# One reciprocal per attention head, head sums of squares on either engine, and weight halves split as separate chains, in a two-layer hybrid trunk

## The chip, the core and the metric

The kernel runs on one core of one Trainium2 chip. A core has five engines, each with its own instruction queue: TensorE (PE, matrix products, the weight load shown as PEld), VectorE (DVE), ScalarE (ACT), GpSimd (POOL) and SyncE (SP, which here only starts transfers). The metric is the device time of one execution in microseconds (us), lower being better.

## The reference

The program is a decoder trunk of two layers on one sequence of 512 tokens with 1024 features, all in fp32. Each layer does the following.

```python
h = rmsnorm(x, norm_g)
p = h @ w_in                                   # 1024 -> 3488 columns, split into 15 parts
q = rope(rmsnorm(rmsnorm(cq) @ w_uq))          # A: latent attention, 4 heads, causal
k, v_a from rmsnorm(ckv) @ w_ukv and kr
o_b = c_b * short_conv(c_c * c_h)              # B: gated width-3 convolution
o_c = sg_u * (tril(sg_w) @ layernorm(sg_v) + sg_b)   # C: chunked spatial gate
qd, kd = rope(rmsnorm(mq)), rope(rmsnorm(mk))  # D: block-sparse attention, 4 heads
o_d = moba(qd, kd, mv)
y = concat(o_a * silu(g_a), o_b * silu(g_b), o_c * silu(g_c), o_d * silu(g_d))
x = x + y @ w_out
```

With 512 tokens and blocks of 256, the block choice of group D selects every earlier block, so it is causal attention too. The per-head norms of q, k, mq and mk need a sum of squares over 64 or 96 values for each token and head. The softmax of each head needs one row sum for each token, and its reciprocal.

## The kernel before, in words

**Precision.** TensorE multiplies in fp32r, a shortened form. Each fp32 operand is split into a high half (the value cast to fp32r) and a low half (value minus high half), and each product is three matmuls: high by high, high by low, low by high (`mm3`, L277). In the names, `whi_` and `wlo_` are the halves of a weight block, `hTh`/`hTl` those of the transposed normalised input, `yTh`/`yTl` those of the gated outputs.

**A planner writes the order.** The Python code runs once, when the program is built, and decides in which order each engine gets its instructions. Class `Order` (L70) has a clock for TensorE (`now`) and one for each of ScalarE (`A`), VectorE (`V`), GpSimd (`G`) and the transfers (`D`). Work is written as generators, "chains" (L162), held in a heap with a due time and a priority (lower goes first). A chain emits an instruction when its inputs are at most 300 ns ahead of `now` (L144, L169), advances the engine's clock by a cost formula (L176 to L194), and goes on. A "lazy" chain also holds back while the engine's own clock is ahead. On the chip, each engine then works strictly through its list, and semaphores hold it where an input is late. Every VectorE, ScalarE and GpSimd instruction is issued in `_emit`, so the profile names line 174 for all of them, and 204 for all matmuls. One reads by tile names.

**TensorE's order of the stages.** In a layer, `main` (L1574) goes through `SEQ` (L364): the low-rank columns (`cq` tiles, weights `c0` to `c3`), `sq`, `ga`, `kv`, then the feature blocks `su`, `gc`, `ch`, `cc`, `gd`, `cb`, `gb`, with the heads' score and value matmuls set between them, and last the output projection. The latter is done in seven block products with sums of weight blocks (`ZPROD`, L46: b11, t3, b21, t4, t2, t1, b22), each of 24 matmuls for an output tile (`prod` and `left` in `main`; results leave through `z_out`, L1544, which adds them to the residual tiles `xr`). The product t1 goes into the bank in which t2's result stood (`oy`), so it starts only when VectorE has added that to `xr`. The left operands of these products are sums of outputs, too, made by VectorE (`ys`, `suml`, `u`).

**Weight blocks ("units").** Each weight block is 128 x 1024 values. `load_units` (L386) loads it on SyncE's queue into a raw tile. There are two such slots (`NRAW`), and the second of each pair of output blocks uses the slots of the rotary scratch. SyncE works in order, so a load that waits for a free slot holds back the loads and copies after it. `split_units` (L417) casts each half of the columns to `whi_` on ScalarE or VectorE, by the planner's clocks, and subtracts on VectorE to get `wlo_`:

```python
yield from c2.act(A.activation, hi, raw, AF.Copy)
...
yield from c2.dve(V.tensor_tensor, lo, raw, hi.bitcast(F32), op=ALU.subtract)
```

For all units but the first four, high and low are made one after the other, first half then second half, and the raw slot is given back (`u.raw_slots.put`) and the unit declared ready at the end. `uq` and `ukv` also carry a gain per row (`split_scaled`, L268). The first four units have the low halves as chains of their own (`low_half`, L456). A product asks for a unit with `unit` (L464), waits for the whole of it, and marks the next `AHEAD` = 4 units as wanted, which lifts the hold on their splits. The sums of weight blocks for t1 to t4 are built in DRAM (`t_sums`, L344): SyncE copies one block, GpSimd's queue adds the other with an accumulating transfer.

**Per-head norms.** `head_means` (L829) squares a whole 128-token tile of q, k, mq or mk on ScalarE into a scratch tile and reduces it to four numbers on VectorE (tiles `squares...` and `rs_...`). When the fourth token tile is done (`L.todo`), GpSimd makes the reciprocal roots.

**Softmax.** For each head and each of its four query tiles, `soft_chain` (L1272) does, on VectorE, the scaled and masked scores and their row minimum, on ScalarE the exponential with the row sum as accumulator, on VectorE the reciprocal of one column, and on ScalarE or VectorE the normalisation. `pt_block` (L1296) then transposes the normalised rows on TensorE, and the halves are split (`pha`, `pla`, `phd`, `pld`).

Of the kernel before, what the change touches and what calls it, by code (L numbers as in the profile page):

```python
# [33 lines left out]
AHEAD = 4  # L34
NWARM, FILL, FILLEND = 6, 0.9, 15000.0
MIXT, MIXLAG, ROWT, COLT = 42000.0, 2000.0, 36000.0, 17500.0
KSPLIT = 6
# [179 lines left out]
def hybrid_trunk(ctx: ExitStack, tc: tile.TileContext, x, positions, norm_g, w_c, w_f, w_t, w_o, mla_q_norm_g,  # L217
# [199 lines left out]
    def split_units(i0, i1):  # L417
        for u in order[i0:i1]:
            ch = Chain(o)
            if u.name != "c0_0":  # L420
                yield from ch.wait(u.loaded)
            u.hi, u.lo = yield from u.slots.get(ch, u.name)
            n = u.a * u.b
            gain = {"uq": 2 * int(u.name[-1]), "ukv": 4 + int(u.name[-1])}.get(u.name[:-2])
            if gain is not None:
                yield from ch.wait(pc_ev)
            for i in range(2):
                if u.name == "c0_0":
# [7 lines left out]
                hi, lo, raw = u.hi[:, sl], u.lo[:, sl], u.raw[:, sl]  # L436
                if gain is not None:
# [33 lines left out]
    LOAD_HOOKS = {}  # L471

# [136 lines left out]
    class Layer:  # L609
        pass  # L610
# [31 lines left out]
    for l in range(DEPTH):  # L642
# [8 lines left out]
        L.todo = {n: NT for n in ("q", "k", "mq", "mk")}  # L651
# [177 lines left out]
    def head_means(ch, L, n, t, z):  # L829

        w = z.shape[2]
        sq = (yield from t2S.get(ch, f"squares{n}{t}"))[:, :4 * w].rearrange("p (h d) -> p h d", h=4)
# [3 lines left out]
        L.todo[n] -= 1  # L836
# [51 lines left out]
    def low_chain(L, t, a, t0, slots):  # L888
# [36 lines left out]
    def q_chain(L, t, q_ps, t0):  # L925
# [13 lines left out]
        if L.todo["q"]:  # L939
            return  # L940
# [11 lines left out]
    def kv_chain(L, t, kv_ps, t0):  # L952
# [23 lines left out]
        if L.todo["k"]:  # L976
# [242 lines left out]
    def mqk_chain(nm):  # L1219
        def f(L, t, a, t0, put):  # L1220
# [11 lines left out]
            if L.todo[nm]:  # L1232
# [39 lines left out]
    def soft_chain(H, qt, s, t0):  # L1272
# [3 lines left out]
        mn = sm.tile([P, 4], F32, tag="mn", name=f"mn{H.name}{qt}")  # L1276
# [3 lines left out]
                          scalar=BIG, op0=ALU.add, op1=ALU.min, accum_out=mn[:, 0:1])  # L1280
# [79 lines left out]
    def heads(L, grp, Vt, prep, qk):  # L1360
        prev = None
        ya_box, ya_left, ya_ev = None, None, None
        for h in range(4):
# [3 lines left out]
            H.rs, H.rs_ev = L.rs[rn], L.rs_ev[rn]  # L1367
            H.soft = [Event() for _ in range(NT)]
# [205 lines left out]
    def main():  # L1574
        m = Chain(o)

        def tok(L, n, width, t, dst, us, k0=0, k1=KT):

            for k in range(k0, k1):
# [61 lines left out]
        def seven(L):  # L1641
# [72 lines left out]
        for L in layers:  # L1714
# [10 lines left out]
            for t in L.torder if l else ():  # L1725
                a = yield from accS.get(m, f"cq{t}_{l}")
                yield from tok(L, "c", 416, t, a[:, 0:416], us)
# [8 lines left out]
            for n in SEQ:  # L1736
                if n in TOKS:
                    us = []
                    for ts in PAIRS.get((n, l), range(NT)):
# [4 lines left out]
                        for k in range(KT):  # L1744
                            for t in ts:
                                yield from tok(L, n, 512, t, a[t], us, k, k + 1)
# [166 lines left out]
```

## Time and profile before

| what | value |
|---|---|
| time, median of 3 runs | 494.73 us (493.85 to 496.37) |
| the profiled execution's own time | 494.88 us |
| its span in the profile | 493.2 us |
| TensorE busy | 486.3 us, 99% |
| VectorE busy | 389.6 us, 79% |
| ScalarE busy | 296.6 us, 60% |
| GpSimd busy | 93.9 us, 19% |
| granted TensorE clock | 1.00 |
| instructions | 7371 |

Span is the time from the first to the last instruction in the profile; the execution's own time is 1.7 us longer. A row of the timeline gives start and duration in us, engine, line, operation, the tile written and the tiles read, the shape, the number of instructions that stand together in the row, and in brackets the idle time of the engine just before it with what ended it. A row of the groups gives the total, and the mean in ns of one instruction. Durations of matmuls overlap, so their pace is read from the starts.

### The profile page before, as it was taken

The page shows a single profiled execution, that of the slowest core. Times are in us where ns is not written, and L with a number is a line of the kernel's source. Part 1 is how long each engine was busy: PE and PEld are TensorE (multiplying, and loading weights), DVE is VectorE, ACT ScalarE, POOL GpSimd, SP SyncE. Part 2 cuts the span into 40 slices and gives each one's busy share as a digit, 9 for nine tenths or more (in the row PEclk, how much of TensorE's full clock was granted, in tenths as well). Part 3 has the DMA queues.
Part 4 walks back from the last instruction along what each step waited for, and adds up shares of the span by engine and source line. Part 5 has one row for each costly group of instructions (what it writes and reads, how often), then busy time and mean ns, then how long its engine had stood idle before and what let it go on. Part 6 is the DMA issues. An engine that isn't in the chain of part 4 may idle for free.

```text
span 493.2 us, 7371 instructions
## 1 busy us (share of the span) xinstructions
PE 486.3 (99%) x2456; PEld 412.8 (84%) x2456; DVE 389.6 (79%) x922; ACT 296.6 (60%) x729; POOL 93.9 (19%) x164
## 2 busy tenths in 40 slices
PE   8999999999999999999999999999999999999997
PEld 7988888888888888888789988888888888888886
DVE  3588788679899888889896777787988878665982
ACT  6788437566557666457476753576746777534730
POOL 7835422100131000000131127040004010000000
PEclk9999999999999999999999999999999999999999
DMA  8525322536493829995564352639149275574562
GB/s 261 192 70 153 121 86 86 128 120 158 152 231 120 182 65 298 238 396 201 181 205 130 90 201 63 202 91 166 64 179 246 88 207 114 182 260 171 204 207 86
DMA packets 36557, 81.33 MB, mean 165 GB/s; under 512 B 6806, under 2 KB 18600, under 8 KB 36264
## 3 DMA queue, kind: packets, MB, share of 16 engines
q1 hardware_dynamic: 28048, 72.48, 43.2%
q0 software_dynamic: 8448, 8.39, 11.3%
q8 instruction: 19, 0.31, 0.3%
q14 instruction: 18, 0.15, 0.1%
q10 hardware_dynamic: 24, 0.01, 0.0%
HBM read 73.00 MB, written 24.64 MB: 198 GB/s over the span
## 4 chain that ended last, share of the span: by engine, by line
PE 86%; DVE 4%; DMA 4%; ACT 2%; issue 1%; SPq 1%; POOL 0%; ACTq 0%; DVEq 0%; POOLq 0%
PE kv L204 10%; PE sq L204 9%; PE cq L204 5%; PE oy L204 5%; PE ch L204 5%; PE cb L204 5%; PE gd L204 4%; PE gb L204 4%; PE cc L204 4%; PE ga L204 4%; PE su L204 4%; PE gc L204 3%; PE sa L204 3%; PE ox L204 2%; PE oz L204 2%; PE sd L204 2%
## 5 line engine op out<-in xcount | busy, mean ns | idle before, releaser
L356 POOL DMA_DIRECT2D t<-in_w_o_dram x16 | 17.2, 1146 | 72.4 <-DMA t<-t 46.5
L174 ACT ACTIVATE pa<-pa,mna 128x256 f32<-128x256 f32 (+3 forms) x48 | 25.8, 549 | 8.2 <-DVE mna L174 8.0
L174 ACT ACTIVATE pd<-pd,mnd 128x256 f32<-128x256 f32 (+3 forms) x50 | 26.7, 549 | 3.5 <-DVE mnd L174 3.5
L204 PE MATMUL kv<-whi_kv,hTh 128*128 128x512 f32 x64 | 27.0, 421 | 0.0
L174 ACT ACTIVATE pha<-pTa 128x512 fp32r<-128x512 f32 (+3 forms) x32 | 14.0, 438 | 21.0 <-PE pTa L204 20.8
L174 ACT ACTIVATE phd<-pTd 128x512 fp32r<-128x512 f32 (+3 forms) x32 | 13.7, 435 | 19.6 <-PE pTd L204 19.5
L204 PE MATMUL kv<-whi_kv,hTl 128*128 128x512 f32 x64 | 25.2, 393 | 0.0
L204 PE MATMUL kv<-wlo_kv,hTh 128*128 128x512 f32 x64 | 25.0, 391 | 0.0
L204 PE MATMUL cq<-whi_c,hTh 128*128 128x416 f32 x64 | 20.9, 371 | 0.8 <-ACT hTh L174 0.8
L174 DVE TENSOR_TENSOR pla<-pTa,pha 128x512 fp32r<-128x512 f32 (+3 forms) x32 | 15.4, 485 | 7.5 <-ACT pha L174 7.5
L174 DVE TENSOR_TENSOR wlo_t<-raw_t,whi_t 128x512 fp32r<-128x512 f32 x32 | 21.0, 685 | 0.0
L174 DVE TENSOR_TENSOR pld<-pTd,phd 128x512 fp32r<-128x512 f32 (+3 forms) x32 | 15.3, 486 | 7.2 <-ACT phd L174 7.1
L204 PE MATMUL cq<-wlo_c,hTh 128*128 128x416 f32 x64 | 20.0, 359 | 0.0
L204 PE MATMUL cq<-whi_c,hTl 128*128 128x416 f32 x64 | 19.8, 355 | 0.0
L174 DVE CUSTOM_DVE_ANT_0 pa<-sa,maskb,rs_q 128x512 f32<-128x512 f32 (+3 forms) x32 | 17.0, 545 | 3.3 <-PE pTa L204 2.1
L174 DVE CUSTOM_DVE_ANT_0 pd<-sd,maskb,rs_mq 128x512 f32<-128x512 f32 (+3 forms) x32 | 16.8, 544 | 2.7 <-PE pTd L204 2.5
L204 PE MATMUL sq<-yTh,hTh 128*128 128x512 f32 x48 | 18.9, 394 | 0.0
L204 PE MATMUL sq<-yTl,hTh 128*128 128x512 f32 x48 | 18.7, 390 | 0.0
L204 PE MATMUL sq<-yTh,hTl 128*128 128x512 f32 x48 | 18.7, 389 | 0.0
L174 ACT ACTIVATE whi_t<-raw_t 128x512 fp32r<-128x512 f32 x32 | 18.2, 618 | 0.6 <-DMA raw_t<-t 0.6
L174 DVE TENSOR_TENSOR wlo_b<-raw_b,whi_b 128x512 fp32r<-128x512 f32 x24 | 15.9, 686 | 1.7 <-ACT whi_b L174 1.7
L174 POOL TENSOR_TENSOR rs_mk<-rs_mk,nhalf 128x16 f32<-128x16 f32 x2 | 6.2, 3112 | 56.3 <-DVE rs_mk L174 56.3
(415 smaller groups left out, 1739.6 us busy)
## 6 DMA issues: line engine op xcount, KB each, us to landing
t<-in_w_o_dram POOLq DMA_DIRECT2D x16, 512.0 KB, 8.5
raw_t<-t SPq DMA_DIRECT2D x16, 512.0 KB, 5.0
raw_b<-in_w_o_dram SPq DMA_DIRECT2D x12, 512.0 KB, 4.7
raw_sq<-in_w_t_dram SPq DMA_DIRECT2D x8, 512.0 KB, 4.0
raw_kv<-in_w_t_dram SPq DMA_DIRECT2D x8, 512.0 KB, 3.6
t<-in_w_o_dram SPq DMA_DIRECT2D x8, 512.0 KB, 5.8
t<-t SPq DMA_DIRECT2D x8, 512.0 KB, 5.2
ys<-ysc SPq DMA_DIRECT2D x14, 256.0 KB, 5.5
```

The lines of the kernel that those rows point to most:

```text
L174: f(*a, **k)
L204: f(*a, **k)
L356: nc.gpsimd.dma_start(z_src(l, n, j), quad(l, b, j), accum_op=ALU.add, max_dma_last_dim=1024)
```

## The change

There are three parts.

1. In `soft_chain`, the row sums of a head's four query tiles lie side by side in one tile (`H.mn`). The query tile whose exponential is the last issues one reciprocal of 128 x 4, and all four normalisations wait for it (`H.rc_ev`).
2. `head_means` waits in the planner until its instructions are nearly due, and then chooses by the planner's clocks: if ScalarE's clock is behind VectorE's (`HMEAN` = 0), four squares with accumulator on ScalarE, one for each head, and no reduce; otherwise the old pair. `L.last` counts the tiles in place of `L.todo`.
3. In `split_units`, every unit's low halves are chains of their own, with priority 5 (the first four units keep -5). While the planner's VectorE clock is more than `VSLACK` = 300 ns ahead of `now` and the unit is more than `URGENT` = 2 units behind the one that TensorE is at, the subtraction is put off. Consumers wait for the half that they use, and the raw slot is given back when both halves are done. `split_scaled` is no longer used there: the gain goes through the same code.

```diff
-AHEAD = 4
+AHEAD, URGENT, VSLACK = 4, 2, 300.0
-KSPLIT = 6
+KSPLIT, HMEAN = 6, 0.0
...
                 if gain is not None:
                     c = gain + (i if u.a == 2 else 0)
-                    yield from split_scaled(c2, hi, lo, raw, pcol[:, c:c + 1])
-                    continue
+                    g = pcol[:, c:c + 1]
                 if o.clk["V"] + 600.0 < o.clk["A"] and u.idx > 3 or u.idx == 0 and i == 0:
-                    yield from c2.dve_fast(V.tensor_copy, hi, raw)
+                    if g is None:
+                        yield from c2.dve_fast(V.tensor_copy, hi, raw)
+                    else:
+                        yield from c2.dve(V.tensor_scalar, hi, raw, g, None, op0=ALU.mult)
                 else:
-                    yield from c2.act(A.activation, hi, raw, AF.Copy)
-                if u.idx < 4:
-                    o.set(u.high[i], c2.t)
-                    o.spawn(low_half(u, i, c2, lo, raw, hi), None, LOPRIO)
-                    continue
-                yield from c2.dve(V.tensor_tensor, lo, raw, hi.bitcast(F32), op=ALU.subtract)
-            if u.idx < 4:
-                continue
-            ch.t = c2.t
-            u.raw_slots.put(ch)
-            o.set(u.ready, ch.t)
-
-    def low_half(u, i, ch, lo, raw, hi):
-        yield from ch.dve(V.tensor_tensor, lo, raw, hi.bitcast(F32), op=ALU.subtract)
+                    yield from c2.act(A.activation, hi, raw, AF.Copy, scale=1.0 if g is None else g)
+                o.set(u.high[i], c2.t)
+                o.spawn(low_half(u, i, c2, lo, raw, hi, g), None, LOPRIO if u.idx < 4 else 5)
+                ch.t = max(ch.t, c2.t - LAT)
+
+    def low_half(u, i, ch, lo, raw, hi, g):
+        while o.clk["V"] > o.now + VSLACK and u.idx > at[0] + URGENT:
+            yield o.now + 100.0
+        ch.t = max(ch.t, o.now)
+        if g is None:
+            yield from ch.dve(V.tensor_tensor, lo, raw, hi.bitcast(F32), op=ALU.subtract)
+        else:
+            yield from ch.dve(V.scalar_tensor_tensor, lo, in0=raw, scalar=g, in1=hi.bitcast(F32),
+                              op0=ALU.mult, op1=ALU.subtract)
         o.set(u.half[i], ch.t)
...
     def unit(ch, name, half=None):
         u = units[name]
+        at[0] = max(at[0], u.idx)
...
     class Layer:
-        pass
+        def last(self, n, ch):
+
+            self.got[n].append(ch.t)
+            ch.t = max(self.got[n])
+            return len(self.got[n]) < NT
...
     def head_means(ch, L, n, t, z):
 
         w = z.shape[2]
+        while max(ch.t, o.clk["A"]) > o.now + SLACK:
+            yield max(ch.t, o.clk["A"]) - SLACK
+        if o.clk["A"] + HMEAN < o.clk["V"]:
+            for h in range(4):
+                yield from ch.act(A.activation, junk[:, :w], z[:, h, :], AF.Square, scale=w ** -0.5,
+                                  accum_out=L.rs[n][:, t, h:h + 1])
+            return
...
-        L.todo[n] -= 1
...
-        uq_h, uq_l = yield from unit(ch, f"uq_{l}")
         for k in range(2):
+            uq_h, uq_l = yield from unit(ch, f"uq_{l}", k)
...
-        yield from ch.act(A.activation, pr, pr, AF.Exp, scale=-1.0, bias=mn[:, 0:1], accum_out=mn[:, 1:2])
-        yield from ch.dve(V.reciprocal, mn[:, 2:3], mn[:, 1:2])
+        yield from ch.act(A.activation, pr, pr, AF.Exp, scale=-1.0, bias=mn[0], accum_out=mn[1])
+        H.exps.append(ch.t)
+        if len(H.exps) == NT:
+            ch.t = max(H.exps)
+            yield from ch.dve(V.reciprocal, H.mn[:, 2, :], H.mn[:, 1, :])
+            o.set(H.rc_ev, ch.t)
+        yield from ch.wait(H.rc_ev)
         if o.clk["A"] + 0.4 * n < o.clk["V"]:
-            yield from ch.act(A.activation, pr, pr, AF.Copy, scale=mn[:, 2:3])
+            yield from ch.act(A.activation, pr, pr, AF.Copy, scale=mn[2])
         else:
-            yield from ch.dve_fast(V.tensor_scalar, pr, pr, mn[:, 2:3], None, op0=ALU.mult)
+            yield from ch.dve_fast(V.tensor_scalar, pr, pr, mn[2], None, op0=ALU.mult)
...
-                if len(us) == k // 2:
-                    us.append((yield from unit(m, f"{n}{k // 2}_{L.l}")))
-                wh, wlo = us[k // 2]
+                wh, wlo = yield from unit(m, f"{n}{k // 2}_{L.l}", k % 2)
...
-                    if (n, kk // 2) not in us:
-                        us[n, kk // 2] = yield from unit(m, f"{n}{kk // 2}_{l}")
-                    wh, wlo = us[n, kk // 2]
+                    wh, wlo = yield from unit(m, f"{n}{kk // 2}_{l}", kk % 2)
...
-                    wh, wlo = yield from unit(m, f"{n}_{l}")
                     for k in range(KT):
+                        wh, wlo = yield from unit(m, f"{n}_{l}", k // 4)
```

More of the change, by code (lines that the diff above doesn't have):

```diff
@@ L471, in hybrid_trunk @@
     LOAD_HOOKS = {}
+    at = [0]
     def shared(slots, n):
@@ L650, in hybrid_trunk @@
         L.qd, L.kd, L.vd = Event(), Event(), [Event() for _ in range(NT)]
-        L.todo = {n: NT for n in ("q", "k", "mq", "mk")}
+        L.got = {n: [] for n in ("q", "k", "mq", "mk")}
         L.stat = [Event() for _ in range(NT)]
@@ L938, in q_chain @@
         yield from head_means(ch, L, "q", t, Q[:, t])
-        if L.todo["q"]:
+        if L.last("q", ch):
             return
@@ L975, in kv_chain @@
         yield from head_means(ch, L, "k", t, K[:, t, :, 0:64])
-        if L.todo["k"]:
+        if L.last("k", ch):
             return
@@ L1231, in f @@
             yield from head_means(ch, L, nm, t, dst[:, t])
-            if L.todo[nm]:
+            if L.last(nm, ch):
                 return
@@ L1275, in soft_chain @@
         pr = yield from pS[qt].get(ch, f"p{H.name}{qt}")
-        mn = sm.tile([P, 4], F32, tag="mn", name=f"mn{H.name}{qt}")
+        if H.mn is None:
+            H.mn = sm.tile([P, 3, NT], F32, tag="mn", name=f"mn{H.name}")
+        mn = [H.mn[:, i, qt:qt + 1] for i in range(3)]
         yield from ch.wait(H.rs_ev)
@@ L1279, in soft_chain @@
                           scale=H.rs[:, qt, H.h:H.h + 1],
-                          scalar=BIG, op0=ALU.add, op1=ALU.min, accum_out=mn[:, 0:1])
+                          scalar=BIG, op0=ALU.add, op1=ALU.min, accum_out=mn[0])
         sS.put(ch)
-        yield from ch.act(A.activation, pr, pr, AF.Exp, scale=-1.0, bias=mn[:, 0:1], accum_out=mn[:, 1:2])
-        yield from ch.dve(V.reciprocal, mn[:, 2:3], mn[:, 1:2])
+        yield from ch.act(A.activation, pr, pr, AF.Exp, scale=-1.0, bias=mn[0], accum_out=mn[1])
[5 more added lines that the diff above has]
+        yield from ch.wait(H.rc_ev)
         if o.clk["A"] + 0.4 * n < o.clk["V"]:
-            yield from ch.act(A.activation, pr, pr, AF.Copy, scale=mn[:, 2:3])
+            yield from ch.act(A.activation, pr, pr, AF.Copy, scale=mn[2])
         else:
-            yield from ch.dve_fast(V.tensor_scalar, pr, pr, mn[:, 2:3], None, op0=ALU.mult)
+            yield from ch.dve_fast(V.tensor_scalar, pr, pr, mn[2], None, op0=ALU.mult)
         H.pr[qt] = pr
@@ L1367, in heads @@
             H.rs, H.rs_ev = L.rs[rn], L.rs_ev[rn]
+            H.mn, H.exps, H.rc_ev = None, [], Event()
             H.soft = [Event() for _ in range(NT)]
@@ L1575, in main, with tok @@
         m = Chain(o)
-        def tok(L, n, width, t, dst, us, k0=0, k1=KT):
+        def tok(L, n, width, t, dst, k0=0, k1=KT):
             for k in range(k0, k1):
@@ L1726, in main @@
                 a = yield from accS.get(m, f"cq{t}_{l}")
-                yield from tok(L, "c", 416, t, a[:, 0:416], us)
+                yield from tok(L, "c", 416, t, a[:, 0:416])
                 o.spawn(low_chain(L, t, a, o.now + PELAT, accS))
@@ L1745, in main @@
                             for t in ts:
-                                yield from tok(L, n, 512, t, a[t], us, k, k + 1)
+                                yield from tok(L, n, 512, t, a[t], k, k + 1)
                         for t in ts:
```

1 line of the change is left out of this document (added).

## The prediction

> **What bounds the kernel now.** I read the busy line of the page first, then its waits of TensorE, then the windows, then the timeline wherever TensorE's cadence breaks.
>
> ```profile
> span 493.2 us, 7371 instructions
> PE 486.3 (99%) x2456; PEld 412.8 (84%) x2456; DVE 389.6 (79%) x922; ACT 296.6 (60%) x729; POOL 93.9 (19%) x164
> ...
> PE 86%; DVE 4%; DMA 4%; ACT 2%; issue 1%; SPq 1%; POOL 0%; ACTq 0%; DVEq 0%; POOLq 0%
> ```
>
> TensorE is busy for 99% of the span, and the chain that ended last is 86% TensorE. A matmul's own duration overlaps its neighbours, so the useful number is the distance from start to start. These two rows of TensorE's timeline stand next to each other in the output stage:
>
> ```profile
> 215.65 0.39 PE L204 MATMUL oz<-whi_b,yTl 128*128 128x512 f32 x1
> 215.88 0.39 PE L204 MATMUL ox<-whi_t,yTh 128*128 128x512 f32 x1
> ```
>
> A 512-column matmul starts 0.23 us after the one before it, and this cadence holds nearly everywhere. The change keeps the set of TensorE instructions, so only starts later than the cadence can be won back. The waits of TensorE by releaser are all there is beside small re-fills:
>
> ```profile
> PE warm L1827 <- DVE ones L1825: 1.1, 1, 1.1
> PE cq L204 <- ACT hTh L174: 0.8, 3, 0.3
> PE hT L204 <- DVE hTl L174: 0.7, 1, 0.7
> PE kv L204 <- ACT Q L174: 0.4, 1, 0.4
> ```
>
> They come to 3.0 us (columns: total, times, longest). What is left to win is small; what can be lost has no such bound. The windows (20 us each: width, then busy time of PE, PEld, DVE, ACT, POOL, then clock, DMA share, GB/s) tell where a second engine is full:
>
> ```profile
> 20.00:40.00 20.00, 19.57 (x106) 17.42 (x106) 15.68 (x43) 16.92 (x63) 11.75 (x25) 1.00 0.29 88
> 200.00:220.00 20.00, 20.00 (x92) 16.52 (x91) 17.03 (x29) 10.44 (x19) 0.00 (x0) 1.00 1.01 332
> 220.00:240.00 20.00, 19.91 (x87) 15.95 (x86) 19.37 (x39) 12.79 (x29) 0.00 (x0) 1.00 0.59 200
> ```
>
> VectorE is full (19.37 of 20) in layer 0's output stage, ScalarE is nearly so at 20 to 40 us, and the DMA engines are full at 200 to 220 us. There the order of instructions decides. Elsewhere both have room.
>
> **The change part by part.** I compared the instruction order of both kernels on each engine. TensorE, GpSimd and SyncE hold the same instructions; VectorE has 58 fewer (924 to 866) and ScalarE 54 more (621 to 675).
>
> *Reciprocals.* 64 of one column become 16 of four columns.
>
> ```profile
> L174 DVE RECIPROCAL mnd<-mnd 128x1 f32<-128x1 f32 x32 | 4.6, 154 | 0.6 <-ACT pd L174 0.6
> ```
>
> That takes 48 x 0.154 = 7.4 us off VectorE at most. It adds a wait: the normalisation of every query tile now waits for the last of the head's four exponentials. Behind it stand the normalised rows that TensorE transposes. In both orders TensorE has other matmuls between a head's last score and its first transpose: summed at the cadence, 4.4 us at least before, 5.1 at least after. The chain that must fit in is row minimum, exponential, reciprocal, normalisation; no wait on `pa` or `pd` stands among TensorE's waits. From the rows of those forms (VectorE's `pa<-sa,maskb,rs_q` 0.55 on average, normalisation on ScalarE 0.72, an exponential taken as long as that at 0.72, reciprocal 0.15) it is 2.1 us, with the accumulator read of the rows below 2.4. Cost nothing; if the cover went, it would cost what exceeds 5.1.
>
> ```profile
> L174 ACT ACTIVATE pa<-pa,mna 128x512 f32<-128x512 f32 x11 | 7.9, 719 | 5.3 <-DVE mna L174 5.3
> L174 DVE CUSTOM_DVE_ANT_0 pa<-sa,maskb,rs_q 128x512 f32<-128x512 f32 (+3 forms) x32 | 17.0, 545 | 3.3 <-PE pTa L204 2.1
> ```
>
> *Sums of squares.* 22 of the 32 square-and-reduce pairs become four small squares with accumulator on ScalarE. The reduce leaves VectorE, the large square leaves ScalarE, and 88 small ones of 64 or 96 columns come. The nearest rows:
>
> ```profile
> L174 DVE TENSOR_REDUCE rs_q<-squaresq 128x4 f32<-128x384 f32 x8 | 4.3, 543 | 0.1
> L174 ACT ACTIVATE squaresq<-Q 128x384 f32<-128x384 f32 x8 | 4.1, 520 | 0.0
> L174 ACT ACTIVATION_READ_ACCUMULATOR junk<-cq 128x1 f32 x24 | 5.1, 210 | 0.0
> L174 ACT ACTIVATE junk<-cq 128x128 f32<-128x128 f32 x8 | 2.2, 278 | 0.1
> L174 ACT ACTIVATE junk<-cq 128x32 f32<-128x32 f32 x8 | 1.6, 199 | 0.1
> ```
>
> Up to 22 x 0.54 = 12 us leave VectorE. A small square costs between 0.199 and 0.278, with its read (0.210) some 0.45 us. So at most 88 x 0.45 - 22 x 0.52 = 28 us more go to ScalarE, which then stands near 325 of 493 us. [...] For the end I take nothing, because ScalarE idles 40% of the span; ScalarE falling behind is a rival below.
>
> *Low halves and their order.* The split of a weight block into high and low halves is now four chains; consumers wait per half. The amount of work is equal; what moves is when. Four places answer.
>
> (a) First stage, ScalarE's timeline and then TensorE's:
>
> ```profile
> 13.21 0.99 ACT L174 ACTIVATE whi_c<-raw_c 128x416 fp32r<-128x416 f32 x2 [0.85 <-DMA raw_c<-in_w_c_dram]
> ...
> 14.51 0.67 ACT L174 ACTIVATE hTh<-xT,pg 128x512 fp32r<-128x512 f32 x1
> 15.23 1.03 PE L204 MATMUL cq<-whi_c,hTh 128*128 128x416 f32 x4 [0.25 <-ACT hTh L174]
> ```
>
> Two `whi_c` halves stand ahead of the `hTh` that TensorE waits for. In the new order only one does. That would put `hTh` half of 0.99 - 0.10 earlier (0.45), but the one before it is anchored to the landing of raw_c at 13.2, and another small square stays. I take -0.35, between 0 and -0.8 (the whole waiting time on `hTh`).
>
> (b) The first key/value product waits for ScalarE's copy of q:
>
> ```profile
> 33.87 0.51 ACT L174 ACTIVATE Q<-q 128x384 f32<-128x384 f32 x1
> 33.62 0.39 PE L204 MATMUL sq<-yTh,hTl 128*128 128x512 f32 x1
> 34.43 0.50 PE L204 MATMUL kv<-whi_ukv,cTh 128*128 128x512 f32 x1 [0.42 <-ACT Q L174]
> ```
>
> 34.43 - 33.62 - 0.23 = 0.58 us lost. In the new order that copy stands ahead of several squares and casts, and adding ScalarE's rows up to it puts it near 32, before TensorE wants its bank. I take -0.58; ends -0.58 and +1.0 (should four small squares, 4 x 0.45 less 0.8 of shadow, get ahead of it).
>
> (c) The first low half of the late `sq` weight block:
>
> ```profile
> 42.84 0.69 DVE L174 TENSOR_TENSOR wlo_sq<-raw_sq,whi_sq 128x512 fp32r<-128x512 f32 x1
> 42.77 0.80 PE L204 MATMUL sq<-whi_sq,hTh 128*128 128x512 f32 x1
> 43.41 0.40 PE L204 MATMUL sq<-wlo_sq,hTh 128*128 128x512 f32 x1
> ```
>
> 43.41 - 42.77 - 0.23 = 0.41 lost. Afterwards its raw slot is freed some 2 us earlier, so both halves are done by 41.8 by the sum of VectorE's rows. I take -0.41; ends -0.41 and 0.
>
> (d) Output stage of layer 0. TensorE's product t1 adds into a bank that VectorE must read first (`xr<-xr,oy`). VectorE has no gap between these two:
>
> ```profile
> 221.62 0.68 DVE L174 TENSOR_TENSOR xr<-xr,ox 128x512 f32<-128x512 f32 x1
> 222.21 0.42 DVE L174 TENSOR_TENSOR ys<-ys 128x256 f32<-128x256 f32 x1
> ...
> 237.33 1.38 DVE L174 TENSOR_TENSOR xr<-xr,oy 128x512 f32<-128x512 f32 x2
> 237.59 0.39 PE L204 MATMUL oy<-whi_t,suml 128*128 128x512 f32 x1
> 238.07 0.50 PE L204 MATMUL oy<-whi_t,sumh 128*128 128x512 f32 x1
> ```
>
> The next instruction starts 0.59 us after one of 512 columns; the one of 256 takes 0.335 in a row. Before, 31 instructions stand from the first `xr` (included) to the second, 15.7 us by these distances, as measured (237.33 - 221.62 = 15.71). After, 33 stand there: two `wlo_t` and one `suml` of 512 and one `ys` of 256 come in, two `wlo_b` of 512 go behind: +0.60 + 0.335 = +0.94. TensorE already waits here (238.07 - 237.59 - 0.23 = 0.25), so all of it shows: +0.94. The ends are 0 (if VectorE had slack, or enters this stretch earlier) and +1.9 (if the last `suml`, also later, adds its own stall).
>
> (e) Elsewhere low halves are made nearer to their use. Matmul time between the last result VectorE needs and the first use falls from about 20 us to 13 to 17 in the feature products, and for the third `kv` block of layer 0 from 10.7 to 3.7 us. What is queued behind is the release of raw slots, and so SyncE's loads, in order. In front of the DMA-full window the t4 sum's copy stands behind raw_t loads:
>
> ```profile
> 190.01 1.94 SPq L290 DMA_DIRECT2D raw_t<-t  x2
> 192.00 0.47 SPq L350 DMA_DIRECT2D t<-t  x1
> ...
> 212.78 2.19 SPq L290 DMA_DIRECT2D raw_t<-t  x2
> ```
>
> GpSimd accumulates onto that copy:
>
> ```profile
> 198.83 1.13 POOL L356 DMA_DIRECT2D t<-in_w_o_dram  x1 [6.89 <-DMA t<-t]
> t<-in_w_o_dram POOLq DMA_DIRECT2D x16, 512.0 KB, 8.5
> ```
>
> From 198.83 and 8.5 us to land that is 207.3, against the reader's issue at 212.78: 5.5 us of slack. By my sums the slot is freed 3 to 4 us later. Cost 0; ends 0 and +3.
>
> (f) Layer change. The 0.72 us wait for `hTl` hangs on GpSimd's norm after TensorE's own products: unchanged, ±0.5. The end of layer 1 repeats (d), but there `xr` has 1.7 us of slack and the list adds about 0.9: nothing.
>
> Sum: -0.35 - 0.58 - 0.41 + 0.94 = -0.40. The profiled run took 494.88 us (span 493.2 and 1.7 around it), 0.15 above the median of 494.73, so 494.88 - 0.40 = 494.5 us.
>
> **Rivals.** *Only the gains* (a to c, d not lost because VectorE enters the stage ahead with up to 19 us less work over the kernel): -1.3, at best all 3.0 us of waits but the 1.1 at the start: 493.0 to 493.6. For it: VectorE loses 58 instructions. Against it: the stretch in (d) begins with an `xr` that TensorE itself releases, so earlier savings don't carry in.
>
> *Slower: low halves too late.* In (e) TensorE meets a `wlo` or a raw block that isn't there. The place is the third and fourth `kv` block and the t blocks, in each layer. The decision comes when VectorE runs more than about 1.6 us behind my sums at `kv` (3.7 us less a cast like that of `hTh`, 0.67, and two subtractions of 0.69), or SyncE more than 5.5 us at t4. The price is 1 to 3 us at each of the four places: two of them give 494.5 + 4 = 498.5. For it: the planner's clock, not the chip, decides how long a low half is put off. Against it: VectorE has idle time in most windows.
>
> *ScalarE late.* The fixed price of the 88 small squares, by the rows above, puts ScalarE behind where it is full (20 to 40 us, 16.92 of 20): +1.0 at (b) in each layer instead of -0.58, 494.5 + 2.6 = 497.1. [...] Against it: the rows of the new order have the copy of q ahead of them.
>
> *It does nothing to the end*: the waits move, 494.9. This lies within the forecast.
>
> **How the numbers follow.** Half a per cent, 2.5 us, is about what a measurement can tell from no change here. Forecast with the "nothing" case, 492.9 to 496.5: 0.60. Only gains: 0.17, a third of it below 492.3, should the 0.25 of (d) and re-fills go too. Low halves late: 0.17, two thirds of it above 497.2. ScalarE late: 0.06, half above. Faster: 0.17 / 3 and 0.05 of the forecast's own for gains that I can't see, 0.11. Slower: 0.11 + 0.03 and 0.04 of the forecast's own for unseen stalls, 0.18. The rest, 0.71, is the same. The range, 492.4 to 498.0, reaches from (a) to (c) with one more wait gone, to 3.5 us of new stalls, and leaves out about 2 in 10.
>
> **What the changed profile would show.** Right: no `kv <- ACT Q` wait among TensorE's; `wlo_sq` before 42 us; TensorE's wait before t1 near 1.2 us at about 238 us; `pTa` and `pTd` free of waits; ScalarE near 320 us busy and VectorE near 375. Wrong: a TensorE wait on a `wlo` tile or on a DMA of more than 1 us, above all at `kv` or in the t products, or ScalarE's squares ahead of an exponential that TensorE then waits for.

## The result and the profile after

The changed kernel takes 498.34 us (median of 13 runs, 496.19 to 501.34) against 494.73 us before: ratio 1.0073, 95% interval 1.0053 to 1.0093. It is slower by 3.6 us. The forecast was 494.5 us, with a range to 498.0.

The top of the page of the changed kernel, and its waits of TensorE (columns: total us, times, longest):

```profile
span 496.6 us, 7465 instructions
PE 488.3 (98%) x2456; PEld 414.4 (83%) x2456; DVE 384.7 (77%) x864; ACT 310.6 (63%) x871; POOL 94.7 (19%) x164
PEclk9999999999989999999999999999999999999999
```

```profile
PE sd L204 <- ACT mk0d L174: 2.3, 1, 2.3
PE warm L1846 <- DVE ones L1844: 1.1, 1, 1.1
PE oy L204 <- DVE xr L174: 1.1, 1, 1.1
PE sq L204 <- DVE yTl L174: 0.4, 1, 0.4
PE ox L204 <- DVE wlo_t L174: 0.2, 1, 0.2
```

The engines did get the work that the change gives them (VectorE 389.6 to 384.7 us, ScalarE 296.6 to 310.6). The waits on `hTh`, `hTl` and `Q` are gone from TensorE's list in this profile. In their place stand four others, and one slice of the clock row shows 8 in place of 9. To see how much each place costs, I summed by how much each matmul starts later than the pace allows. The pace is the usual distance from the start before it: 0.2275 us after a matmul of 512 columns, 0.190 of 416, 0.175 of 384, 0.118 of 256, 0.1085 of 128 (each within 0.001 us of the median of these distances in both kernels):

| stretch, us | predicted | lost before | lost after | difference |
|---|---|---|---|---|
| 0 to 17, start | -0.35 | 3.70 | 2.78 | -0.92 |
| 30 to 36, copy of q | -0.58 | 0.76 | 0.36 | -0.40 |
| 36 to 46, `sq` | -0.41 | 0.61 | 1.18 | +0.57 |
| 135 to 160, first scores of group D | 0 | 0.29 | 4.27 | +3.98 |
| 160 to 232 | 0 | 0.43 | 0.98 | +0.55 |
| 232 to 242, t1 | +0.94 | 0.53 | 1.31 | +0.78 |
| 242 to 262, layer change | 0 | 0.98 | 0.14 | -0.84 |
| the rest | 0 | 2.18 | 2.27 | +0.09 |

The differences sum to +3.8 us, and TensorE's last matmul starts 3.8 us later (at 493.0 instead of 489.2 us); what comes after it is 0.4 us shorter, so the span grows by 3.4. One stretch, 135 to 160 us, holds as much as the whole loss. It divides into a pause and a slow spell. These are the windows of the changed kernel across it (width, busy time of PE, PEld, DVE, ACT, POOL, then the granted clock, the DMA share and GB/s):

```profile
142.00:144.00 2.00, 0.06 (x1) 0.00 (x0) 1.19 (x3) 1.05 (x2) 0.00 (x0) 1.00 1.18 292
144.00:146.00 2.00, 1.68 (x8) 1.48 (x9) 0.34 (x1) 1.58 (x3) 0.00 (x0) 0.96 0.38 145
146.00:148.00 2.00, 2.00 (x6) 1.58 (x5) 1.97 (x6) 1.44 (x4) 0.00 (x0) 0.50 0.00 0
148.00:150.00 2.00, 2.00 (x8) 1.63 (x8) 1.31 (x6) 1.25 (x6) 0.42 (x1) 0.69 0.04 8
150.00:152.00 2.00, 2.00 (x11) 1.72 (x11) 2.00 (x4) 1.96 (x5) 0.10 (x1) 1.00 0.00 0
```

TensorE stands still for 2.3 us. Then, from 146 to about 149 us, its granted clock is 0.50 (3.4 us in all, by what the three windows from 144 to 150 us lack to 1.00), seven matmuls start 0.43 us apart in place of 0.23, and 1.4 us more are lost.

The cause of the pause can be followed through four engines of the changed kernel, VectorE, SyncE, ScalarE and TensorE:

```profile
133.77 1.28 DVE L174 TENSOR_TENSOR wlo_gd<-raw_gd,whi_gd 128x512 fp32r<-128x512 f32 x2
135.12 0.33 SPq L290 DMA_DIRECT2D raw_gb<-in_w_f_dram  x1
142.93 0.63 ACT L174 ACTIVATE whi_gb<-raw_gb 128x512 fp32r<-128x512 f32 x1 [2.87 <-DMA raw_gb<-in_w_f_dram]
143.58 0.68 ACT L174 ACTIVATE mk0d<-tmkd,pcol 64x512 fp32r<-64x512 f32 x1
144.32 0.50 PE L204 MATMUL sd<-mk0d,mq0d 128*128 128x512 f32 x1 [2.26 <-ACT mk0d L174]
```

The low halves of the second `gd` block are put off to 133.8. Their end frees the raw slot, and SyncE issues the load of `raw_gb` at once, at 135.1. It lands 7.8 us later. ScalarE's list has the cast of that block ahead of `mk0d`, the key layout of the first group D heads, so ScalarE idles 2.87 us with `mk0d` behind it, and TensorE waits for `mk0d`. In the kernel before, the same links were these:

```profile
129.16 0.67 DVE L174 TENSOR_TENSOR wlo_gd<-raw_gd,whi_gd 128x512 fp32r<-128x512 f32 x1
129.86 0.33 SPq L290 DMA_DIRECT2D raw_gb<-in_w_f_dram  x1
140.87 0.62 ACT L174 ACTIVATE whi_gb<-raw_gb 128x512 fp32r<-128x512 f32 x1
142.79 0.68 ACT L174 ACTIVATE mk0d<-tmkd,pcol 64x512 fp32r<-64x512 f32 x1
```

The slot came free 5.3 us earlier, and the load took 4.0 us to land by the profile's view of that tile, in place of 7.8. So the cast, which stood ahead of the last piece of `mk0d` there too, had its data.

### The profile page after: what moved, and what is told of

It is laid out like the page before. It is cut to its first block, busy times and chain, and to the rows that moved or that the text cites. A ratio compares the mean times of both kernels' runs of the same rounds, so it can differ in the third digit from the quotient of the medians.

```text
span 496.6 us, 7465 instructions
## 1 busy us (share of the span) xinstructions
PE 488.3 (98%) x2456; PEld 414.4 (83%) x2456; DVE 384.7 (77%) x864; ACT 310.6 (63%) x871; POOL 94.7 (19%) x164
## 4 chain that ended last, share of the span: by engine, by line
PE 87%; DMA 6%; DVE 4%; ACT 1%; issue 1%; DVEq 0%; SPq 0%; ACTq 0%
PE kv L204 10%; PE sq L204 9%; PE cq L204 7%; PE oy L204 5%; PE cb L204 4%; PE ga L204 4%; PE gd L204 4%; PE ch L204 4%; PE gb L204 4%; PE cc L204 3%; PE su L204 3%; PE gc L204 3%; PE sa L204 3%; PE ox L204 2%; PE oz L204 2%; PE sd L204 2%
## 5 line engine op out<-in xcount | busy, mean ns | idle before, releaser
L174 ACT ACTIVATE pd<-pd,mnd 128x128 f32<-128x128 f32 (+3 forms) x50 | 26.4, 549 | 3.8 <-DVE mnd L174 3.6
L174 ACT ACTIVATE pa<-pa,mna 128x384 f32<-128x384 f32 (+3 forms) x42 | 22.4, 549 | 2.8 <-DVE mna L174 2.8
L204 PEld LDWEIGHTS kv<-whi_kv,hTl 128*128 128x128 f32 x64 | 12.0, 188 | 2.8
```

The source lines that it names most:

```text
L174: f(*a, **k)
L204: f(*a, **k)
```

## The experiments

**Theory 1**: the pause comes from a cast of a late load ahead of `mk0d` on ScalarE, and the clock dip from the pause. Rivals: `mk0d`'s own inputs are late; the dip has a cause of its own; the small squares or the shared reciprocal cost the time.

**One cast moved.** The planner's order is left alone; the instruction is kept back when the program is written and put in after `mk0d`.

```diff
+    held, held_lo = [], []
...
-                    yield from c2.act(A.activation, hi, raw, AF.Copy, scale=1.0 if g is None else g)
+                    first = u.name == "gb0_0" and i == 0
+                    f = (lambda *z, **kw: held.append((z, kw))) if first else A.activation
+                    yield from c2.act(f, hi, raw, AF.Copy, scale=1.0 if g is None else g)
...
                             yield from ch.act(A.activation, w[b0:b1, :], src, AF.Copy, scale=g)
+                            while held:
+                                z, kw = held.pop()
+                                A.activation(*z, **kw)
```

> The changed kernel, with one ScalarE instruction moved: the cast of the first half of whi_gb (layer 0) behind the cast that completes mk0d, which TensorE waits for 2.3 us. Theory 1 (the cast waits for a late raw_gb and holds up mk0d behind it): the wait on mk0d goes, the granted clock stays 1.00 between 146 and 150 us, and 2.4 + 1.4 = 3.8 us go: about 494.5. Theory 2 (mk0d's own inputs are late, the cast beside it is chance): the wait stays near 2.3 us and the time near 498.3. Theory 3 (the clock dips for a reason of its own): the wait goes and the dip stays: about 495.9.

Measured: 497.21 us, ratio 1.0049 (1.0032 to 1.0066). The wait on `mk0d` is gone, but a wait of 1.5 us stands a few matmuls on. The slow spell is gone too, going by the pace: 0.23 us between matmuls of 512 columns after that wait. (The clock column can't tell here, as it reads 0.95 in all ten windows from 142 to 162 us, at the usual pace.) The rows are of VectorE and TensorE in this kernel:

```profile
145.33 0.76 DVE L174 SCALAR_TENSOR_TENSOR kl1d<-tmkd,pcol,mk1d 64x512 fp32r<-64x512 f32 x1 [1.83 <-ACT mk1d L174]
146.12 0.75 DVE L174 CUSTOM_DVE_ANT_0 pd<-sd,maskb,rs_mq 128x512 f32<-128x512 f32 x1
146.93 0.33 PE L204 MATMUL sd<-mk0d,mq0d 128*128 128x128 f32 x1 [1.53 <-DVE mnd L174]
```

The other half of the same cast still stood ahead of `mk1d`. VectorE waited for `mk1d` with the row minima queued behind it, and these free the bank that the fourth score tile needs. So theory 1 holds for the cast, but I had priced the move too high: the same load holds up a second chain, which costs 1.7 us by the pace and had been hidden under the first.

**The pause filled.** Ten matmuls ahead of the score product keep TensorE busy:

```diff
             qs, kd, kl = (pair[k, H.h % 2] for k in ("mq", "mk", "kl"))
+            if H.name == "d00" and qt == 3:
+                hh = hk(L, 0)[0]
+                for _ in range(10):
+                    PE.matmul(s, hh[:, 0:P], hh[:, :512], start=True, stop=True)
```

> The changed kernel, with ten extra matmuls of 512 columns (2.3 us, results overwritten) ahead of the score product that waits for mk0d. They change no result and no other engine's order. Theory 1: TensorE doesn't pause, the clock stays 1.00, and only the 1.4 us lost after the pause come back: about 496.9; the score product starts at the same place. If the dip has another reason: no gain, 498.3. If the extra matmuls themselves cost: up to 500.6.

Measured: 497.62 us, ratio 1.0052 (1.0039 to 1.0065). In its profiled run the cast that makes `mk0d` started 1.2 us later still, so TensorE waited 0.9 us beyond the ten matmuls; the clock stayed at 1.00:

```profile
144.00:146.00 2.00, 1.09 (x5) 0.62 (x4) 0.00 (x0) 1.81 (x3) 0.00 (x0) 1.00 0.70 248
146.00:148.00 2.00, 2.00 (x12) 1.74 (x11) 1.10 (x2) 1.15 (x3) 0.00 (x0) 1.00 0.02 6
```

The stretch 146 to 160 us loses 0.10 there, against 1.60 in the changed kernel.

**The pause put into the kernel before.**

```diff
+                            if x == 0 and H.name == "d00":
+                                for _ in range(5):
+                                    A.activation(w[b0:b1, :], src, AF.Copy, scale=g)
                             yield from ch.act(A.activation, w[b0:b1, :], src, AF.Copy, scale=g)
```

> The kernel before, with five extra copies (the same cast repeated) on ScalarE ahead of mk0d in layer 0: 2.9 us, of which 0.6 is slack. Theory 1: TensorE waits some 2.3 us there, the granted clock dips to about 0.5 afterwards and costs about 1.4 us more: 494.7 + 3.7 = 498.4. If the dip has another reason: 494.7 + 2.3 = 497.0 with the clock at 1.00.

Measured: 500.02 us, ratio 1.0099 (1.0087 to 1.0111). The wait came out at 3.6 us in place of 2.3, and the dip followed here as well, in a kernel that has nothing else of the change:

```profile
148.00:150.00 2.00, 2.00 (x9) 1.72 (x9) 1.94 (x5) 1.11 (x3) 0.00 (x0) 0.67 0.35 123
150.00:152.00 2.00, 2.00 (x6) 1.53 (x5) 2.00 (x6) 2.00 (x6) 0.00 (x0) 0.50 0.34 139
```

It loses 3.7 us more in the stretch 135 to 146 and 1.5 us more from 146 to 160: 5.2 of the 5.2 us measured. So here a pause alone, of 3.6 us, brought the dip.

**Three moves, then four.** Two further stalls of the changed kernel are single instructions in front of the one that TensorE waits for: two `wlo_t` halves before `xr` (t1), and one `wlo_sq` before `yTl` at 40 us. They are kept back in the same manner:

```diff
-            yield from ch.dve(V.tensor_tensor, lo, raw, hi.bitcast(F32), op=ALU.subtract)
+            late = u.name == "t11_0" or u.name == "sq3_0" and i == 0
+            f = (lambda *z, **kw: held_lo.append((z, kw))) if late else V.tensor_tensor
+            yield from ch.dve(f, lo, raw, hi.bitcast(F32), op=ALU.subtract)
...
```

> The changed kernel with three moves of single instructions and no other change: the whi_gb cast behind mk0d (as in gb_swap), in the output stage of layer 0 two wlo_t subtractions of t1 behind the xr that gates t1, and at 40 us one wlo_sq behind the yTl that TensorE waits for. Theory 1 with the sum of the stalls: -3.8, -1.1 and -0.5 against the changed kernel: 498.3 - 5.4 = 492.9, faster than the kernel before by 1.8. If the stalls only move to the next late instruction: 494 to 496.

Measured: 495.18 us, ratio 1.0015 (1.0000 to 1.0029). The stretch 36 to 46 loses 0.60 and 232 to 242 loses 0.22, so both moves took their stalls away; the wait on the row minima (1.4 us) was left, as in the first experiment. Then both halves of the cast went behind both casts of `mk1d`:

```diff
-                    first = u.name == "gb0_0" and i == 0
+                    first = u.name == "gb0_0"
...
-                            while held:
-                                z, kw = held.pop()
+                            while held and x == 1:
+                                z, kw = held.pop(0)
```

> The three moves of all_swaps, and now both halves of the whi_gb cast behind both casts of mk1d, so that neither mk0d nor mk1d (and VectorE's kl1d and the row minima behind it) waits for raw_gb. Theory 1: the wait of 1.5 us on the row minima goes as well, no wait above 0.6 us is left between 130 and 160 us, and the time is 495.2 - 1.6 = 493.6. Rival (the row minima are late for a reason of their own): the wait stays, 495.2.

Measured: 493.07 us (492.10 to 494.23), ratio 0.9963 (0.9949 to 0.9977). This version is faster than both kernels, by 1.6 and 5.3 us. Its span and all of its TensorE waits:

```profile
span 491.2 us, 7466 instructions
```

```profile
PE warm L1863 <- DVE ones L1861: 1.1, 1, 1.1
PE cq L204 <- ACT hTh L174: 0.6, 2, 0.3
PE pTd L204 <- DVE pld L174: 0.3, 1, 0.3
```

Its 2456 matmuls are those of the changed kernel, with all 88 small squares and 16 shared reciprocals. So the loss doesn't come from these; it came from five instructions in the wrong place (two halves of a cast, three subtractions).

**The load that landed late.** GpSimd's accumulating transfers were issued at 132.8 and 134.3 us, just ahead of `raw_gb`; here they are kept back until the memset of the second head pair.

```diff
-                    nc.gpsimd.dma_start(z_src(l, n, j), quad(l, b, j), accum_op=ALU.add, max_dma_last_dim=1024)
+                    if (l, n) == (0, "t3"):
+                        held_acc.append((z_src(l, n, j), quad(l, b, j)))
+                    else:
+                        nc.gpsimd.dma_start(z_src(l, n, j), quad(l, b, j), accum_op=ALU.add, max_dma_last_dim=1024)
...
+                            while held_acc and hp == 1:
+                                z, q = held_acc.pop(0)
+                                nc.gpsimd.dma_start(z, q, accum_op=ALU.add, max_dma_last_dim=1024)
```

> The changed kernel with GpSimd's two accumulating transfers of the t3 sum (issued at 132.8 and 134.3 us, just before the load of raw_gb at 135.1) put some 15 us later; no other order changes. Theory C (the late raw slot and the collision are both needed): raw_gb lands 4 us after its issue, near 139.5, its cast no longer holds up mk0d, the wait of 2.3 us and the clock dip go: about 498.3 - 3.9 = 494.4. Rival (the load is slow by itself or by SyncE's own copies): it lands after 142 us as before and the time stays near 498.

Measured: 499.18 us, ratio 1.0099 (1.0075 to 1.0122). The mechanism is as expected and the time is not. These rows are ScalarE's, SyncE's, VectorE's and TensorE's, with GpSimd's moved transfers:

```profile
140.20 0.63 ACT L174 ACTIVATE whi_gb<-raw_gb 128x512 fp32r<-128x512 f32 x1
140.86 0.68 ACT L174 ACTIVATE mk0d<-tmkd,pcol 64x512 fp32r<-64x512 f32 x1
146.04 2.08 POOL L1487 DMA_DIRECT2D t<-in_w_o_dram  x2
149.36 0.33 SPq L290 DMA_DIRECT2D raw_cc<-in_w_f_dram  x1
156.84 0.43 DVE L174 CAST whi_cc<-raw_cc 128x512 fp32r<-128x512 f32 x1 [3.93 <-DMA raw_cc<-in_w_f_dram]
158.33 0.33 PE L204 MATMUL sd<-mk1d,mq1d 128*128 128x128 f32 x1 [2.61 <-DVE mnd L174]
```

`raw_gb`, issued at 135.2, has landed by 140.2: 5.0 us at most in place of 7.8, and the wait on `mk0d` is gone. In the kernel before, it was issued ahead of these transfers (129.9 against 136.5 and 138.0) and took 4.0. So the late slot alone did not hold up `mk0d`; it took the slow landing as well. But the transfers moved to 146 us now run beside the next load but one, `raw_cc`. That takes 7.5 us, its cast stands on VectorE ahead of row minima, and TensorE waits 2.6 us for the bank. It is the same mechanism at another place. The profiled run took 497.96 us; what the other runs lose beyond it isn't shown. The two transfers are issued by GpSimd and the load by SyncE, and in the changed kernel the packets of both took the 16 DMA engines' time from 130 to 144 us: 51.4% of it for the two transfers' queue and 53.0% for SyncE's, against none and 62.5% here. How the two share an engine isn't shown.

**Each part undone.** First, a reciprocal for each query tile again:

```diff
-            yield from ch.dve(V.reciprocal, H.mn[:, 2, :], H.mn[:, 1, :])
...
+        yield from ch.dve(V.reciprocal, mn[:, 2:3], mn[:, 1:2])
```

> The changed kernel with one reciprocal for each query tile again. In its order the casts of whi_gb stand behind mk0d and mk1d. Theory 1 (the place of the cast against mk0d decides): no wait at mk0d, clock at 1.00, about 498.3 - 4 = 494.3. Rival (the late low halves alone cost it): 498. If the shared reciprocal itself costs time in the heads: below 494.

Measured: 501.52 us, ratio 1.0141 (1.0119 to 1.0163), worse than the changed kernel. In layer 0 the casts do stand behind, and nothing is lost there. But the planner's list differs from there on, and the same chain turns up in layer 1, on `raw_cc`:

```profile
403.75 0.63 ACT L174 ACTIVATE whi_cc<-raw_cc 128x512 fp32r<-128x512 f32 x1 [2.80 <-DMA raw_cc<-in_w_f_dram]
405.14 0.50 PE L204 MATMUL sd<-mk0d,mq0d 128*128 128x512 f32 x1 [2.44 <-ACT mk0d L174]
```

Here, too, the load landed late: issued at 395.7, it took 8.1 us. The wait and the slow spell behind it cost 4.2 us; another 2.8 are lost from 320 to 340 us, where TensorE waits 1.5 us for `pha`, and I did not follow that.

Second, the old square and reduce for every tile:

```diff
-        while max(ch.t, o.clk["A"]) > o.now + SLACK:
-            yield max(ch.t, o.clk["A"]) - SLACK
-        if o.clk["A"] + HMEAN < o.clk["V"]:
-            for h in range(4):
-                yield from ch.act(A.activation, junk[:, :w], z[:, h, :], AF.Square, scale=w ** -0.5,
-                                  accum_out=L.rs[n][:, t, h:h + 1])
-            return
```

> The changed kernel with the old square and reduce for every tile. The cast of whi_gb still stands ahead of mk0d. Theory 1 with a collision (raw_gb took 7.8 us to land because GpSimd's accumulating transfers, which the earlier sums of squares brought forward by 3 us, ran beside it): those transfers start after 135 us again, raw_gb lands in 4 to 5 us, the wait at mk0d is under 0.5 us and the time about 494.7. Rival (the late raw slot alone decides): the wait stays at 2 us or more and the time near 498.

Measured: 498.41 us, ratio 1.0073 (1.0054 to 1.0092), the same as the changed kernel. My expectation fell: the accumulating transfers are issued at 133.3 and 134.8 with the old squares too, `raw_gb` lands at 143.4, and the wait is 2.2 us. The new sums of squares don't bring the collision about, and the time doesn't hang on them. What brought these transfers forward from 136.5 us stays open.

Third, the low halves as before (the whole of that part taken back; this is its core), with the other two parts in:

```diff
-                o.spawn(low_half(u, i, c2, lo, raw, hi, g), None, LOPRIO if u.idx < 4 else 5)
+                yield from c2.dve(V.tensor_tensor, lo, raw, hi.bitcast(F32), op=ALU.subtract)
```

> The kernel before with the shared reciprocal and the new sums of squares, low halves as before. Theory 1: raw slots come free early, no wait above 1 us from 130 to 160 us; the waits at the start (0.8) and on the copy of q come back; about 494.5. Rival (the 88 small squares or the shared reciprocal cost the time): 497 or more.

Measured: 497.58 us, ratio 1.0059 (1.0046 to 1.0072). There is no wait from 130 to 160 us, and the old waits on `hTh`, `hTl` and `Q` are back, as expected. But TensorE waits at another place, where the keys of group A hang on GpSimd's `rs_k`:

```profile
PE t1a L204 <- DVE K L174: 1.7, 1, 1.7
```

The stretch from 46 to 135 us loses 1.9 us more than before by this. The profiled run was the fastest one (496.17, 1.5 above the kernel before); what the others lose beyond it, up to the 2.9 us of the median, is not shown.

**The putting off undone**, for one unit and then for all:

```diff
-        while o.clk["V"] > o.now + VSLACK and u.idx > at[0] + URGENT:
+        while u.name != "gd1_0" and o.clk["V"] > o.now + VSLACK and u.idx > at[0] + URGENT:
```

> The changed kernel with one unit, gd1 of layer 0, excepted from the putting off of low halves. Its raw slot comes free about 5 us earlier, so raw_gb should be issued near 130 us. Theory 1: no wait at mk0d in layer 0, about 494.4. The orders behind it change too, so if other waits take its place (the planner writes another list with the same blind spot), 496 to 500.

Measured: 495.50 us, ratio 1.0017 (1.0002 to 1.0032). `raw_gb` is issued at 130.3, its cast has run by 137.0, and no wait is left from 130 to 160 us. That gives back 2.8 of the 3.6 us; about 1.5 us are lost anew to waits of 0.4 to 1.0 us on `pld`, `wlo_t` and `suml`.

```diff
-AHEAD, URGENT, VSLACK = 4, 2, 300.0
+AHEAD, URGENT, VSLACK = 4, 2, 1e9
```

> The changed kernel with no putting off at all (VSLACK without bound): low halves stay chains of their own by halves. Theory 1 (the putting off is what costs): raw slots come free as early as before, the start and the copy of q keep their gain of about 0.9, the rest as before: 493.5 to 494.5. Rival (the separate chains and the new order cost it, wherever the low halves stand): 497 or more.

Measured: 501.71 us, ratio 1.0143 (1.0121 to 1.0166). `raw_gb` is issued at 128.9 and `mk0d` is on time, but VectorE's list in the output stage is worse, since low halves now stand ahead of `suml` and `xr`:

```profile
PE oy L204 <- DVE suml L174: 2.5, 1, 2.5
PE oy L204 <- DVE wlo_t L174: 2.1, 2, 1.5
PE oz L204 <- DVE wlo_b L174: 1.2, 1, 1.2
```

So putting low halves off isn't bad as such; the halves of one block were put off too far.

**A later landing in the planner's books.**

```diff
-        ch.t = o.clk["D"] + 2000.0
+        ch.t = o.clk["D"] + (2000.0 if o.now < 30000.0 else 5500.0)
```

> The changed kernel with one number of the planner changed: from 30 us on, a load is booked to land 3.5 us later than before (5.5 in place of 2.0 us after its share of the transfer time), near what raw_gb took. Theory 1 (stalls come from casts listed ahead of work that TensorE waits for, because the planner believes in an early landing): waits on mk0d go in both layers, 494 or less. Rival (orders are as good or bad by chance): 496 to 500 with waits at other places.

Measured: 511.57 us, ratio 1.0336 (1.0315 to 1.0358). The casts go behind `mk0d` and the waits on it are gone, but now other blocks are cast late, and TensorE waits for the casts themselves (`sq` on `whi_sq` 2.7 us, `ox` on `whi_t` 2.2). A later estimate for all loads is no cure.

## Why the prediction was wrong, point by point

**Bound: right.** The set of matmuls is the same, little could be won, and the loss came in new waits.

**Reciprocals and sums of squares: right, at nothing.** The fastest version has both. A square of 64 columns took 251 ns and one of 96 columns 285 ns on average, within the bounds of 199 and 278 for the first and just above for the second, and reads 188 to 193 ns. ScalarE ended at 310.6 us, 14 above before, where I had allowed 28 at most. VectorE ended at 384.7, above the 375 that I had named: reciprocals and reduces did shrink, but six normalisations `pa` and some casts came to it from ScalarE.

```profile
L174 ACT ACTIVATE junk<-Q 128x96 f32<-128x96 f32 x24 | 6.8, 285 | 0.5
L174 ACT ACTIVATION_READ_ACCUMULATOR junk<-Q 128x1 f32 x24 | 4.6, 193 | 0.0
L174 DVE RECIPROCAL mnd<-mnd 128x4 f32<-128x4 f32 x8 | 1.4, 174 | 0.2
```

**(a) Start: right in size.** One profile shows -0.92, but the start scatters with the landing of `raw_c` (ScalarE's idle time for it ahead of the `whi_c` casts goes from 0.1 us at most with the transfers later to 1.8 in the kernel before): eleven profiles with the new low halves lose 3.2 us there on average (2.6 to 3.9), three without them 3.5 us. That is about -0.4 against -0.35.

**(b) Copy of q: right.** -0.40 against -0.58; the copy starts at 31.90, where I had put it near 32, and the wait is in no profile with the new low halves.

**(c) First low half of the late `sq` block: misread.** I took 0.41 us between two starts for a wait on `wlo_sq`, though no view of waits named one. It is there after the change too, when that half had been ready for over 2 us:

```profile
39.37 1.02 DVE L174 TENSOR_TENSOR wlo_sq<-raw_sq,whi_sq 128x512 fp32r<-128x512 f32 x1
41.61 1.02 PE L204 MATMUL rrow<-rd,ones 128*128 128x512 f32 x2
42.07 0.80 PE L204 MATMUL sq<-whi_sq,hTh 128*128 128x512 f32 x1
42.70 0.40 PE L204 MATMUL sq<-wlo_sq,hTh 128*128 128x512 f32 x1
```

In the twelve profiles whose rows show them, the matmul behind the two `rrow` starts 0.45 to 0.47 us after the first of them, and the one after that 0.63 to 0.65 us later in the eight whose rows reach so far: 0.4 us over the pace in all. It goes with these two `rrow` matmuls and isn't a wait on `wlo_sq`. And 0.5 us were lost next to it, which I hadn't seen: the same `wlo_sq` now stands ahead of `yTl`.

**(d) Output stage: right.** +1.03 at t1 (0.25 before, 1.28 after), against +0.94; +0.78 over the whole stretch. Putting the two `wlo_t` behind the `xr` took it away.

**(e) "Elsewhere low halves are made nearer to their use ... Cost 0": this step failed.** I named the right link, the release of raw slots and SyncE's loads, and then sized it at one place only, the t4 sum, which had 5.5 us of slack. What had to be asked of every load was when its cast stands in an engine's list, and what TensorE needs stands behind it. `raw_gb` was issued 5.3 us later, and GpSimd's two accumulating transfers came 3.7 us earlier, so that it now went out behind them and took 7.8 us to land in place of 4.0; and its cast stood ahead of `mk0d`. The cost was 4.0 us at this one place, against the 0 in my sum, and my upper end for (e) was 3. The price also lacked the slow clock, 1.4 of these 4.0 us, which I didn't have in the account.

**(f) Layer change: off by 0.84 to the good.** The wait on `hTl` went with the new low halves (in the kernel with the later landing `hT` still waits 0.5 us for it) and stayed in the kernel without them (0.96 us lost from 242 to 262 us, against 0.14). GpSimd's last norm there starts at 253.98 before and at 257.92 after, while TensorE, too, is 3.95 us behind (its transposes at 255.88 and 259.83): in that I was right. But I took the products ahead of it as unchanged. The planner now puts nine `cq` matmuls in place of three ahead of the transposes that wait, and these cover the wait.

**The sum apart from (e).** Without the stretch from 135 to 160 us the differences come to -0.2 us, near my -0.40. Part of that is luck: (c) was off by +0.98 and (f) by -0.84. The +0.55 from 160 to 232 us I did not foresee and have not followed to a cause.

**The rivals.** "Low halves too late" was the right one by name, and its 498.5 us is near, but the place and the sign to look for that I gave were wrong: TensorE waited neither on a `wlo` tile nor on a load, but on `mk0d`, which has nothing to do with weights. I gave it 0.17. ScalarE did fall behind, as the third rival had it, by waiting for a load and not through its small squares.

## What to carry to other kernels

When an edit moves the release of a buffer, follow every load that the buffer gates to the first instruction that reads it, and look at what stands behind that instruction on the same engine: the engine works in order (here ScalarE idled 2.87 us for a cast's load with `mk0d` behind it), and the victim can be unrelated work. Where lists are written ahead from estimated landing times, each edit deals a new list; find the few instructions that gate TensorE and move those, since undoing a part or changing an estimate deals the list again (495.5 to 511.6 us here), while moving five instructions gave 493.07. And price a pause of TensorE with what its clock may lose afterwards (1.4 and 1.5 us in two kernels here).

## What the runs showed of the hardware

A pause of TensorE of 2.3 us was followed by 3.4 us at a granted clock of 0.50, which cost 1.4 us more in the changed kernel; after a pause of 3.6 us put into the kernel before, the same cost 1.5. The slow pace (matmuls of 512 columns 0.43 us apart) also followed waits of 2.2 us (old squares) and 2.4 (a reciprocal for each tile). It isn't a fixed consequence: none followed waits of 1.5 us (one cast moved, by its pace) and 2.6 (transfers later, where the clock reads 1.00 in every window from 142 to 162 us). So the length of the pause alone doesn't tell whether the dip follows, as it did after 2.2 us in one kernel and didn't after 2.6 in another; what decides it isn't shown. The profiled run without putting off, whose longest wait was 2.5 us, has a mean clock of 0.997, like the changed kernel's. That the spread of the changed kernel's runs (496.2 to 501.3) comes from this dip is likely, as its two runs with a mean clock of 1.000 are among its four fastest, but it isn't shown.

The second thing is the landing of a load of 512 KB issued behind accumulating transfers: 6.5 to 8.7 us in these runs (7.8 in the changed kernel), against 4.0 ahead of them and 5.0 at most when they were moved away.
